# Bias rows in 24 spaced copies, one-hot rows cast by GpSimd, wider convolution ends, an earlier weight load

## The chip, the core and the metric

The kernel runs on one core of a Trainium2 chip. The core has TensorE (PE in the profile, with PEld for its weight loads), VectorE (DVE), ScalarE (ACT), GpSimd (POOL) and a sync engine (SP) that issues most of the transfers between device memory and the on-chip memory; 16 DMA engines carry them out. Each engine runs its own list of instructions in order, and waits on semaphores for the others. The metric is the time of one execution in microseconds of the device, a median of runs; lower is better.

## What is computed

One decoder block on a sequence of 1024 tokens of width 1024, in float32. Two mixers run side by side on the normalised input: dilated sliding-window attention in three groups of eight heads, with a bias that depends on the distance, and a convolution over 31 taps. Their results are gated, mixed, and followed by a feed-forward part. What the change touches is the bias and the convolution:

```python
bias = bias_tab[rel_bucket(offset * dilation)].astype(jnp.float32).transpose(2, 0, 1)
s = jnp.einsum('brnqhd,brnkhd->brnhqk', qb, kb).astype(jnp.float32) * (Dh ** -0.5) + bias
...
u, gate = jnp.split(h, 2, axis=-1)
u = u * jax.nn.sigmoid(gate)
u = lax.conv_general_dilated(u, w_dw, ..., feature_group_count=CONV_CHANNELS) + b_dw
u = jax.nn.silu(layer_norm(u, g_ln, b_ln))
return u @ w_conv_out + b_conv_out
```

## The kernel before

Every matrix product is made of two-part numbers: a float32 block is split into a high part, which ScalarE casts, and a low part, the difference, which VectorE or GpSimd computes, and three matmuls of 128x512 take the place of one (L336 to L338, L352 to L354). Most products are further done in the seven-product scheme for 2x2 blocks (`winograd`, `pair`), which needs sums of weight quarters (`quarters`, L214 to L256). So a weight block is loaded by SP (`load_ahead`, L183), split or summed by ScalarE, VectorE and GpSimd, and only then used by TensorE.

The program's order is written out by hand. TensorE's matmuls are emitted in the order of the stages, and after each group of three `tick` is called. At a tick, steps that were put off (`later`) are emitted, and each background generator goes on to its next `yield`; `yield n` lets n ticks pass and goes on at the one after. What a tick emits stands on the queue of its engine in that order, and an engine that waits holds up all that stands behind it. On SP, too, a transfer that waits holds up the transfers behind it.

The stages around the change, in order of time:

- Start, and two gated units on unsplit products; then the normalised input is prepared (`renorm`, `block_sums`) beside one early gate unit and five first halves of gated pairs (`head`, L400). The weight blocks of this stretch are split by `part` (L196 on ScalarE, L197 on VectorE); the first pair's sums are made by L236 and L237 and split by L214 and L215.
- Six gated pairs, whose results `d_u` go to memory (L887); seven pairs of gates; twelve pairs of queries and keys (`qk_pair`, L986 to L1013). Beside them `conv` computes the convolution, one block of 128 channels after the other: 46 products with accumulation (L848 to L853) in three banks, with gaps given by `CONV`; then ScalarE copies a bank (L858, L859), VectorE makes three sums (L861 to L863), the block is stored (L865), and GpSimd later adds it to a running sum (L875). L376, L904 to L917 and L1001 to L1013 empty TensorE's banks on ScalarE and VectorE and stand between these.
- The value projections (L1113, L1114), beside them the layer norm of the convolution (`conv_norm`: L1463 forms the mean from the running sum, L1472 to L1479 subtract, square and add, L469 reduces) and the attention. At its end one gate unit (`plain_gate`) and the convolution's output product with eight weight blocks `w_co`.

`bias_lines`, a background generator of the second stage, makes the bias rows: a one-hot matrix of 33x384 times the bias table gives 8 rows of 384 values per group, a `line`. The line is stored (L536) and expanded by one transfer from memory to memory, which repeats each of its 8 rows 128 times (L539, `rep`, 1.5 MB). The attention loads slanted windows of `rep` from 579 us on (L549).

Of the kernel before, what the change touches and what calls it, by code (L numbers as in the profile page):

```python
# [10 lines left out]
F32R = mybir.dt.float32r  # L11
# [53 lines left out]
class Build:  # L65
# [440 lines left out]
    def bias_lines(self):  # L506

        nc = self.nc
        self.rep = []

        def load(g):
            oh = self.slot(F32R)
            nc.gpsimd.dma_start(oh[0:33, :384], self.p_onehot[g].bitcast(F32R))
            return oh

        nxt = load(0)
        tab = self.half()
        nc.gpsimd.memset(tab[32:33, :24], 1.0)
        nc.gpsimd.dma_start(tab[0:32, :24], self.p_tab)
        yield 8  # L520
        parts = self.half(F32R)
        hi, lo = parts[0:33, :24], parts[0:33, 24:48]
        nc.scalar.copy(hi, tab[0:33, :24])
        nc.vector.tensor_tensor(lo, tab[0:33, :24], f(hi), op=OP.subtract)
        yield 8
        for g in range(3):
            oh, nxt = nxt, load(g + 1) if g < 2 else None
            ps = self.bank()
            for e, part in enumerate((hi, lo)):
                nc.tensor.matmul(ps[0:8, :384], part[:, g * 8:(g + 1) * 8], oh[0:33, :384],  # L530
                                 start=e == 0, stop=e == 1)
            oh = None
            yield 1
            nc.scalar.copy(tab[64:72, :384], ps[0:8, :384])
            line = self.dram.tile([8, 384], F32, name=f"line{g}")
            nc.sync.dma_start(line, tab[64:72, :384])  # L536
            rep = self.dram.tile([8, 128, 384], F32, name=f"rep{g}")
            yield 10
            nc.sync.dma_start(rep, bass.AP(tensor=line.tensor, offset=line.offset,  # L539
                                           ap=[[384, 8], [0, 128], [1, 384]]))  # L540
            self.rep.append(rep)
            yield 14
# [263 lines left out]
    def conv(self):  # L806
# [3 lines left out]
        nc = self.nc  # L810
# [14 lines left out]
        nxt, src = fetch(0), None  # L825
        yield 0

        for b in range(8):
# [27 lines left out]
            src = ahead  # L856
            o = self.slot()
            nc.scalar.copy(s, A[0])  # L858
            nc.scalar.copy(o[:, 0:1], A[0][:, 0:1])  # L859
            yield 1  # L860
            nc.vector.tensor_tensor(o[:, 1:H], s[:, 1:], A[1][:, :H - 1], op=OP.add)  # L861
            nc.vector.tensor_tensor(s, s, A[1], op=OP.add)
            nc.vector.tensor_tensor(o[:, H:], A[2], s, op=OP.subtract)  # L863
# [19 lines left out]
    cg, CONV = 0, (0, 1, 0, 0, 0, 1)  # L883
# [799 lines left out]
def build(ctx, tc, aps):  # L1683
    B = Build(ctx, tc, aps)
    nc = B.nc
# [73 lines left out]
    def plain_gate(n, job, early):  # L1759
        if early:  # L1760
            B.queue_split(job)
            B.flush(job)
            w = B.hl.pop(job)
        else:
            w = B.timed([job], co[:1], 3, 9)[0]
        for hf in range(2):
# [591 lines left out]
```

## Time and profile before

| what | value |
|---|---|
| median of three runs | 1688.18 us (1686.38 to 1690.43) |
| profiled execution | 1687.09 us, span 1685.3 us |
| granted TensorE clock in it | 0.999 |

The span goes from the first to the last instruction of the profiled execution. A row of the timeline gives start and length in us, engine, line, operation and tiles, how many instructions it stands for, and in brackets the idle time ahead of it with what ended it. A row of a window gives the busy time of TensorE, its weight loads, VectorE, ScalarE and GpSimd, then the clock, the share of the DMA engines and GB/s. TensorE's busy time is modelled from its instructions, so its gaps are read from the idle times.

### The profile page before, as it was taken

The numbers are of one execution on the slowest core, as the hardware profiler recorded it, in microseconds if no ns is written. First come the engines' busy times: TensorE is split into PE (matmuls) and PEld (weight loads), VectorE is DVE, ScalarE is ACT, GpSimd is POOL, SyncE is SP. The second block draws the span as 40 slices with busy tenths as digits, with TensorE's granted clock in tenths as the row PEclk, the third lists the DMA queues.
The fourth block names the chain that finished last, engine by engine and source line by source line (L and its number), as shares of the span: only waits on it lengthen the run. The fifth ranks groups of instructions, "written<-read, shape, count | busy, mean of one in ns | idle before, by whom it ended". The sixth has DMA issues, their size and how long they took to land.

```text
span 1685.3 us, 23529 instructions
## 1 busy us (share of the span) xinstructions
PE 1668.1 (99%) x8119; PEld 1393.9 (83%) x8119; DVE 1277.7 (76%) x2268; ACT 827.6 (49%) x1646; POOL 522.2 (31%) x408
## 2 busy tenths in 40 slices
PE   9999999999999999999999999999999999999998
PEld 7778888888878889999888888888888888888886
DVE  6899988888988767778885846877655566676686
ACT  7354334343444588888822447643333333354453
POOL 0028777888777165665300300000000000000000
PEclk9999999999999999999999999999999999999999
DMA  4443343355656888779998624234133222494334
GB/s 182 164 165 138 110 140 119 138 186 174 197 166 171 269 269 236 225 233 256 308 274 316 198 88 153 74 131 150 69 107 118 94 94 106 170 374 126 111 121 156
DMA packets 164641, 289.66 MB, mean 172 GB/s; under 512 B 47534, under 2 KB 79273, under 8 KB 164521
## 3 DMA queue, kind: packets, MB, share of 16 engines
q1 hardware_dynamic: 163832, 287.56, 52.6%
q8 instruction: 64, 1.05, 0.3%
q0 software_dynamic: 544, 0.34, 0.1%
q14 instruction: 57, 0.46, 0.1%
q10 hardware_dynamic: 144, 0.26, 0.0%
HBM read 197.39 MB, written 95.42 MB: 174 GB/s over the span
## 4 chain that ended last, share of the span: by engine, by line
PE 67%; DMA 3%; DVE 1%; ACT 1%; issue 0%; SPq 0%; DVEq 0%; POOL 0%; POOLq 0%; ACTq 0%
PE p L2242 12%; PE p L353 10%; PE p L354 10%; PE p L352 10%; PE p L1986 5%; PE p L1113 5%; PE p L1114 3%; PE p L336 2%; PE p L338 2%; PE p L337 2%; PE p L1229 2%; PE p L1300 2%; PE p L1267 1%; DMA b<-dk 1%; DMA b<-dq 1%; DMA b<-dv 0%
## 5 line engine op out<-in xcount | busy, mean ns | idle before, releaser
L352 PE MATMUL p<-b,b 128*128 128x512 f32 x1316 | 513.6, 390 | 3.5 <-ACT b L214 1.7
L354 PE MATMUL p<-b,b 128*128 128x512 f32 x1316 | 512.8, 390 | 0.9 <-DVE b L215 0.5
L353 PE MATMUL p<-b,b 128*128 128x512 f32 x1316 | 512.2, 389 | 0.1
L352 PEld LDWEIGHTS p<-b,b 128*128 128x128 f32 x1316 | 247.0, 188 | 58.6 <-ACT b L214 2.1
L354 PEld LDWEIGHTS p<-b,b 128*128 128x128 f32 x1316 | 247.0, 188 | 54.4 <-DVE b L197 1.5
L353 PEld LDWEIGHTS p<-b,b 128*128 128x128 f32 x1316 | 247.1, 188 | 51.4 <-DVE b L1437 0.5
L2242 PE MATMUL p<-b,b 128*128 128x512 f32 x924 | 209.6, 389 | 0.0
L2242 PEld LDWEIGHTS p<-b,b 128*128 128x128 f32 x924 | 173.5, 188 | 36.0
L853 DVE SCALAR_TENSOR_TENSOR p<-b,par,p 128x511 f32<-128x511 f32 (+14 forms) x232 | 163.2, 738 | 0.0
L1113 PE MATMUL p<-b,b 128*128 128x512 f32 x384 | 144.1, 407 | 0.0
L214 ACT CAST b<-d 128x1024 fp32r<-128x1024 f32 x82 | 86.2, 1051 | 97.3 <-POOL d L237 54.5
L215 POOL TENSOR_TENSOR b<-d,b 128x1024 fp32r<-128x1024 f32 x43 | 104.6, 2433 | 50.7 <-ACT b L214 38.9
L1437 DVE TENSOR_TENSOR b<-b,b 128x512 fp32r<-128x512 f32 x141 | 98.8, 707 | 16.9 <-ACT b L1436 15.3
L215 DVE TENSOR_TENSOR b<-d,b 128x1024 fp32r<-128x1024 f32 x39 | 47.6, 1220 | 79.3 <-ACT b L214 79.3
L1114 PE MATMUL p<-b,b 128*128 128x256 f32 x384 | 107.7, 280 | 0.0
L1436 ACT CAST b<-b 128x512 fp32r<-128x512 f32 x141 | 86.4, 619 | 39.7 <-PE p L2242 18.1
L336 PE MATMUL p<-b,b 128*128 128x512 f32 x240 | 96.1, 401 | 0.0
L338 PE MATMUL p<-b,b 128*128 128x512 f32 x240 | 93.6, 390 | 0.0
L337 PE MATMUL p<-b,b 128*128 128x512 f32 x240 | 93.6, 390 | 0.0
L214 ACT CAST b<-b 128x1024 fp32r<-128x1024 f32 x51 | 53.6, 1052 | 80.4 <-POOL b L246 36.5
L1242 ACT ACTIVATE c<-c,stat 128x128 f32<-128x128 f32 (+1 forms) x192 | 85.2, 448 | 14.6 <-DVE stat L1232 13.3
L1986 PE MATMUL p<-b,b 128*128 128x512 f32 x384 | 90.0, 392 | 0.0
(245 smaller groups left out, 2879.1 us busy)
## 6 DMA issues: line engine op xcount, KB each, us to landing
b<-w_in SPq DMA_DIRECT2D x33, 512.0 KB, 5.0
b<-w_fi SPq DMA_DIRECT2D x29, 512.0 KB, 5.0
d<-w_in SPq DMA_DIRECT2D x25, 512.0 KB, 4.4
dk<-c SPq DMA_DIRECT2D x48, 256.0 KB, 4.1
dq<-c SPq DMA_DIRECT2D x48, 256.0 KB, 3.8
b<-dq SPq DMA_DIRECT2D x48, 256.0 KB, 5.6
b<-dk SPq DMA_DIRECT2D x48, 256.0 KB, 7.3
d<-w_fi SPq DMA_DIRECT2D x22, 512.0 KB, 4.1
```

What stands on the lines that cost most here:

```text
L214: self.nc.scalar.copy(hi, x)
L215: self.wsplit.tensor_tensor(lo, x, f(hi), op=OP.subtract)
L336: nc.tensor.matmul(ps, hi[:, s], a, start=kt == 0, stop=False)
L337: nc.tensor.matmul(ps, hi[:, s], b, start=False, stop=False)
L352: nc.tensor.matmul(ps, hi[:, s], a, start=first and kt == 0, stop=False, skip_group_check=True)
L353: nc.tensor.matmul(ps, hi[:, s], b, start=False, stop=False, skip_group_check=True)
L354: nc.tensor.matmul(ps, lo[:, s], a, start=False, stop=kt == 3, skip_group_check=True)
L853: nc.vector.scalar_tensor_tensor(A[i][:, j:], src[i][:, :H - j], w[i], A[i][:, j:], op0=OP.mult, op1=OP.add)
L1113: nc.tensor.matmul(ps, a, w, start=kt == 0, stop=kt == KT - 1, skip_group_check=True)
L1114: nc.tensor.matmul(ps[:, 256:], b, w[:, :256], start=False, stop=kt == KT - 1, skip_group_check=True)
L1986: nc.tensor.matmul(banks[tt][nh], st, wt[:, nh * H:(nh + 1) * H], start=bool(kt == 0 and a), stop=bool(kt == KT - 1 and b))
L2242: nc.tensor.matmul(acc[t], x, y, start=first and e == 0, stop=last and e == 2, skip_group_check=True)
```

## The change

Four edits. `bias_lines` loads its one-hot rows by SP as float32 into smaller tiles, and GpSimd casts them to the type that TensorE takes, where before GpSimd's own queue loaded them straight into tiles of that type. It stores the three lines early, frees its tiles, lets 60 ticks pass, and then expands each line in eight transfers of one row each, four ticks apart. `conv` lets three ticks pass ahead of the copies of a finished bank, three ahead of the sums, and puts the sums on ticks of their own; the gaps between its products are shorter on average at first (`CONV` as set in the class; the list set for the query and key pairs stays). In `plain_gate` the load of the second `w_co` block is set to 14 ticks after the start of the late gate unit.

```diff
-        def load(g):
-            oh = self.slot(F32R)
-            nc.gpsimd.dma_start(oh[0:33, :384], self.p_onehot[g].bitcast(F32R))
-            return oh
-
-        nxt = load(0)
+        oh = []
+
+        def load(g):
+            x = self.half()
+            nc.sync.dma_start(x[0:33, :384], self.p_onehot[g])
+            oh.append(x)
+
+        load(0)
         tab = self.half()
         nc.gpsimd.memset(tab[32:33, :24], 1.0)
         nc.gpsimd.dma_start(tab[0:32, :24], self.p_tab)
-        yield 8
+        yield 6
...
-        yield 8
+        load(1)
+        lines = []
         for g in range(3):
-            oh, nxt = nxt, load(g + 1) if g < 2 else None
+            x, y = oh.pop(0), self.half(F32R)
+            nc.gpsimd.tensor_copy(y[0:33, :384], x[0:33, :384])
+            x = None
+            if g == 0:
+                load(2)
+            yield 5
             ps = self.bank()
             for e, part in enumerate((hi, lo)):
-                nc.tensor.matmul(ps[0:8, :384], part[:, g * 8:(g + 1) * 8], oh[0:33, :384],
+                nc.tensor.matmul(ps[0:8, :384], part[:, g * 8:(g + 1) * 8], y[0:33, :384],
                                  start=e == 0, stop=e == 1)
-            oh = None
-            yield 1
+            y = None
+            yield 2
             nc.scalar.copy(tab[64:72, :384], ps[0:8, :384])
+            ps = None
             line = self.dram.tile([8, 384], F32, name=f"line{g}")
             nc.sync.dma_start(line, tab[64:72, :384])
+            lines.append(line)
+        tab = parts = hi = lo = line = part = None
+        yield 60
+        for g, line in enumerate(lines):
             rep = self.dram.tile([8, 128, 384], F32, name=f"rep{g}")
-            yield 10
-            nc.sync.dma_start(rep, bass.AP(tensor=line.tensor, offset=line.offset,
-                                           ap=[[384, 8], [0, 128], [1, 384]]))
+            for h in range(8):
+                nc.sync.dma_start(rep[h], bass.AP(tensor=line.tensor, offset=line.offset + h * 384,
+                                                  ap=[[0, 128], [1, 384]]))
+                yield 3
             self.rep.append(rep)
-            yield 14
...
             src = ahead
+            yield 2
             o = self.slot()
             nc.scalar.copy(s, A[0])
             nc.scalar.copy(o[:, 0:1], A[0][:, 0:1])
-            yield 1
+            yield 2
             nc.vector.tensor_tensor(o[:, 1:H], s[:, 1:], A[1][:, :H - 1], op=OP.add)
+            yield 0
             nc.vector.tensor_tensor(s, s, A[1], op=OP.add)
+            yield 0
             nc.vector.tensor_tensor(o[:, H:], A[2], s, op=OP.subtract)
...
-    cg, CONV = 0, (0, 1, 0, 0, 0, 1)
+    cg, CONV = 0, (0,0,0,1)
...
             w = B.timed([job], co[:1], 3, 9)[0]
+            B.later(14, lambda: B.load_ahead(co[1]))
```

The edits add lines, so the change's line numbers are higher: L515 and L531 load and cast the one-hot rows, L545 stores a line and L552 expands it, L829 is the old L816 and L903 the old L887; L866 is a tap, L875, L877 and L879 are the three sums, L881 the block's store, and the old L986 to L1013 are 16 higher.

SP's queue in the stretch of the five first halves, before: `line`, then weight blocks, and the expansion of group 0 between them.

```order
L1737 DMA du_90<-b_603 128x1024
L183 DMA b_727<-w_in 128x1024
L536 DMA line_748<-c_632 8x384
L887 DMA dgc_128<-c_763 128x512
L183 DMA b_774<-w_in 128x1024
L539 DMA rep_750<-line_748 1024x1x384
L887 DMA dgc_128<-c_803 128x512
L816 DMA b_806<-du_89 128x1024
L183 DMA b_823<-w_in 128x1024
L183 DMA b_878<-w_in 128x1024
L183 DMA d_900<-w_in 128x1024
```

The same place now:

```order
L1753 DMA du_90<-b_603 128x1024
L545 DMA line_734<-c_632 8x384
L183 DMA b_741<-w_in 128x1024
L903 DMA dgc_128<-c_771 128x512
L183 DMA b_782<-w_in 128x1024
L545 DMA line_786<-c_632 8x384
L903 DMA dgc_128<-c_818 128x512
L829 DMA b_821<-du_89 128x1024
L183 DMA b_838<-w_in 128x1024
L545 DMA line_845<-c_632 8x384
L183 DMA b_896<-w_in 128x1024
L183 DMA d_918<-w_in 128x1024
```

The expansion has gone from here, and all three lines are stored here. The first of the new transfers stand behind the store of `d_u` block 2, among the weight blocks of the gated pairs:

```order
L903 DMA du_91<-c_1190 128x512
L552 DMA rep_1223<-line_734 128x384 x3
L183 DMA d_1280<-w_in 128x1024
L183 DMA b_1282<-w_in 128x1024
L552 DMA rep_1223<-line_734 128x384 x2
L903 DMA du_92<-c_1194 128x512
L903 DMA du_92<-c_1316 128x512
L552 DMA rep_1223<-line_734 128x384 x2
L829 DMA b_1378<-du_90 128x1024
```

From here on they go on in this way, one to four together, to the last gated pair.

VectorE's queue at the end of a convolution block among the query and key pairs (in the trace at 407 to 414 us), before:

```order
L987 TENSOR_TENSOR c_3602<-c_3602,c_3625 128x512
L861 TENSOR_TENSOR b_3620<-c_3039,p_3127 128x511
L862 TENSOR_TENSOR c_3039<-c_3039,p_3127 128x512
L863 TENSOR_TENSOR b_3620<-p_3128,c_3039 128x512
L850 TENSOR_SCALAR p_3643<-b_3371,par 128x512
L848 TENSOR_SCALAR p_3644<-b_3371,par 128x512
L850 TENSOR_SCALAR p_3645<-c_3572,pairs,bias_551 128x512
L1007 TENSOR_TENSOR c_3671<-p_3548,c_3552 128x128x4
```

And the end of the same block now:

```order
L1003 TENSOR_TENSOR c_3702<-c_3702,c_3721 128x512
L1029 SCALAR_TENSOR_TENSOR c_3725<-p_3567,c_3724 128x128x4
L875 TENSOR_TENSOR b_3748<-c_3126,p_3228 128x511
L877 TENSOR_TENSOR c_3126<-c_3126,p_3228 128x512
L879 TENSOR_TENSOR b_3748<-p_3229,c_3126 128x512
L1017 TENSOR_TENSOR c_3781<-p_3729,c_3730 128x128x4
L863 TENSOR_SCALAR p_3786<-b_3486,par 128x512
L861 TENSOR_SCALAR p_3787<-b_3486,par 128x512
L1003 TENSOR_TENSOR c_3781<-c_3781,c_3805 128x512
L863 TENSOR_SCALAR p_3788<-c_3670,pairs,bias_551 128x512
```

The block ends later against the pairs, and instructions that empty TensorE's banks (L1017) stand between the sums and the first products of the next block. At another block the order is again sums, one product, then L1023, the old L1007.

VectorE's queue at the end of the last block, before; behind it come a pair without taps and then the value projections:

```order
L853 SCALAR_TENSOR_TENSOR p_4164<-c_4086,par,p_4164 128x497
L1007 TENSOR_TENSOR c_4649<-p_4535,c_4539 128x64x8
L861 TENSOR_TENSOR b_4654<-c_4086,p_4163 128x511
L862 TENSOR_TENSOR c_4086<-c_4086,p_4163 128x512
L863 TENSOR_TENSOR b_4654<-p_4164,c_4086 128x512
L990 SCALAR_TENSOR_TENSOR c_4649<-c_4649,c_4669 128x512
L1001 TENSOR_TENSOR c_4672<-p_4607,c_4538 128x64x8
L987 TENSOR_TENSOR c_4672<-c_4672,c_4690 128x512
L1013 SCALAR_TENSOR_TENSOR c_4694<-p_4535,c_4693 128x64x8
```

And now, up to the last L1029 (the old L1013) ahead of the value projections:

```order
L866 SCALAR_TENSOR_TENSOR p_4336<-c_4231,par,p_4336 128x497
L208 TENSOR_TENSOR b_4817<-b_4728,b_4817 128x2x256
L1023 TENSOR_TENSOR c_4820<-p_4707,c_4711 128x64x8
L208 TENSOR_TENSOR b_4837<-b_4730,b_4837 128x2x256
L1006 SCALAR_TENSOR_TENSOR c_4820<-c_4820,c_4840 128x512
L1017 TENSOR_TENSOR c_4843<-p_4779,c_4710 128x64x8
L875 TENSOR_TENSOR b_4831<-c_4231,p_4335 128x511
L877 TENSOR_TENSOR c_4231<-c_4231,p_4335 128x512
L208 TENSOR_TENSOR b_4859<-b_4730,b_4859 128x2x256
L879 TENSOR_TENSOR b_4831<-p_4336,c_4231 128x512
L1003 TENSOR_TENSOR c_4843<-c_4843,c_4863 128x512
L1029 SCALAR_TENSOR_TENSOR c_4867<-p_4707,c_4866 128x64x8
```

The last block now ends in the last pair instead of the one before it: 15 taps that stood ahead of the old end of the block, and the three sums, stand between the last L1007 of the pair before and the last L1013. GpSimd's addition of the block, L875 before, stands behind them. On SP, the store of block 7 stood well ahead of the loads for the layer norm and now stands behind the first of them; and the second `w_co` block, which stood behind two `dq` loads, a store and two `dact` loads, now stands ahead of them.

## The prediction

> **What bounds the kernel now.** I read the page's head and the busy time by window first, then TensorE's own timeline for every gap, and from each gap back to what released it.
>
> ```profile
> span 1685.3 us, 23529 instructions
> PE 1668.1 (99%) x8119; PEld 1393.9 (83%) x8119; DVE 1277.7 (76%) x2268; ACT 827.6 (49%) x1646; POOL 522.2 (31%) x408
> ...
> 50.00:100.00 50.00, 47.41 (x201) 35.88 (x199) 44.81 (x73) 22.46 (x40) 1.04 (x2) 1.00 0.51 181
> 400.00:500.00 100.00, 98.51 (x430) 80.09 (x429) 91.29 (x118) 41.18 (x60) 79.85 (x46) 1.00 0.59 180
> 800.00:900.00 100.00, 97.57 (x526) 81.72 (x525) 82.62 (x177) 46.59 (x132) 17.83 (x23) 1.00 1.00 290
> ```
>
> TensorE is the bound: it is busy for 1668.1 of 1685.3 us and the change keeps every large matmul. So only its 17.2 us of gaps can be won. Three windows hold most of what lies inside the program: 2.59, 1.49 and 2.43 us (window minus the PE column). These are the gaps themselves; the bracket gives the idle time and its releaser:
>
> ```profile
> 89.39 0.50 PE L354 MATMUL p<-b,b 128*128 128x512 f32 x1 [0.28 <-DVE b L197]
> 96.67 0.50 PE L352 MATMUL p<-b,b 128*128 128x512 f32 x1 [1.67 <-ACT b L214]
> 97.92 0.50 PE L354 MATMUL p<-b,b 128*128 128x512 f32 x1 [0.53 <-DVE b L215]
> ...
> 413.37 0.50 PE L352 MATMUL p<-b,b 128*128 128x512 f32 x1 [0.59 <-DVE c L1007]
> 468.63 0.50 PE L352 MATMUL p<-b,b 128*128 128x512 f32 x1 [0.56 <-ACT c L376]
> 472.00 0.50 PE L352 MATMUL p<-b,b 128*128 128x512 f32 x1 [0.35 <-DVE c L1007]
> ...
> 809.99 0.39 PE L1300 MATMUL p<-c,b 128*128 128x256 f32 x1 [1.02 <-ACT c L1274]
> ```
>
> **Part A, the bias rows: 2.5 us won.** The first three gaps have one cause, a late weight block.
>
> ```profile
> 66.05 0.77 SPq L539 DMA_DIRECT2D rep<-line  x1
> 71.77 0.89 SPq L183 DMA_DIRECT2D b<-w_in  x2
> 81.98 0.62 ACT L196 CAST b<-b 128x512 fp32r<-128x512 f32 x1 [5.17 <-DMA b<-w_in]
> 82.63 0.69 DVE L197 TENSOR_TENSOR b<-b,b 128x512 fp32r<-128x512 f32 x1 [4.23 <-ACT b L196]
> 94.07 0.69 DVE L236 TENSOR_TENSOR d<-b 128x512 f32<-128x512 f32 x1
> 95.57 1.04 ACT L214 CAST b<-d 128x1024 fp32r<-128x1024 f32 x1 [3.10 <-DVE d L237]
> b<-w_in SPq DMA_DIRECT2D x33, 512.0 KB, 5.0
> ```
>
> The load issued at 71.77 lands at 81.98, 10.2 us later, where such loads take 5.0 in the median. ACT waits 5.17 us for it, VectorE 4.23 behind ACT. VectorE's queue is then full; L236 runs late, L214 and L215 behind it, and TensorE stands 0.28 + 1.67 + 0.53 = 2.48 us. What the load met is the 1.5 MB expansion issued at 66.05. The change takes all three expansions out of this stretch. The load then lands near 76.8, when ACT had finished its earlier work (81.98 - 5.17). I take 2.5; the ends are 0 (something else holds the load) and the window's 2.59.
>
> What it adds there: three 49.5 KB loads behind the first store of `du`, on a queue that then waits for VectorE anyway; three line stores, each a queue entry ahead of a weight load; and three GpSimd casts, on an engine that was busy 1.04 us in the whole window. A 64-row cast of 512 columns gives an upper price:
>
> ```profile
> 805.70 0.60 POOL L1053 CAST b<-b 64x512 fp32r<-64x512 f32 x1
> ```
>
> By the code's gaps a one-hot load stands seven ticks ahead of its cast and the cast six ticks ahead of its matmul. A tick is three matmuls, 0.69 us by the second window (3 x 98.51 / 430), so load and cast have 8.9 us together; a 512 KB load lands in 5.0 and the cast takes 0.6 at most. Nothing is charged; if the cover went, a late cast would cost TensorE up to its 0.6 us.
>
> The 24 pieces now run from about 113 us on, 3 to 8 per pair of weight blocks, each one queue entry of 196 KB. While an old expansion ran, the DMA engines looked like this (85 to 100 us, forty slices):
>
> ```profile
> DMA  1000000555559955589999995555545455410000
> ```
>
> Half of the engines are busy for some 29 slices of 0.375 us, 10.9 us, where nothing is added. A piece is an eighth of that work: 1.4 us at this rate. By the code a weight block is loaded there 15 ticks, 10 us, ahead of its first cast and lands in 5.0, so three pieces in front are absorbed: 0 charged. Nothing waits for the pieces themselves before the attention, some 400 us on. The upper end is that the stall of A returns once, 2.5. The Trainium skill, page "DMA: Bandwidth & Descriptors", section "Why a DMA increments its semaphore by 16 and not by 1", says a copy runs on as many engines, up to 16, as divide the slowest dimension of both sides: 8 for the old form, 16 for a piece. The half-busy row agrees; by the rule a piece takes 0.7 us instead of 1.4, which leaves the sum alone and lowers the chance of the second rival below.
>
> **Part B, the convolution's ends: 1.1 us won.** At a block's end ACT copies a finished bank (L858) and VectorE adds three times without a pause.
>
> ```profile
> 412.28 1.04 DVE L1007 TENSOR_TENSOR c<-p,c 128x512 f32<-128x512 f32 x1
> 467.44 0.59 ACT L858 COPY c<-p 128x512 f32<-128x512 f32 x1 [2.24 <-DVE p L853]
> 467.98 0.60 ACT L376 COPY c<-p 128x512 f32<-128x512 f32 x1
> 470.88 1.06 DVE L1007 TENSOR_TENSOR c<-p,c 128x512 f32<-128x512 f32 x1
> ```
>
> At 467 the copy had been queued before its last tap was done; L376, which frees TensorE's bank, stood 2.24 us behind it: 0.56 us of TensorE. At 412 and 471 L1007 stood behind the three sums and the next block's first products: 0.59 and 0.35. The three extra ticks ahead of the copy remove the first kind; spacing the sums lets L1007 in between, though the change's order still has one block where L1007 follows the sums directly. Of 1.50 I take 1.1; ends 0 and 1.5.
>
> **Part C, the second w_co load: 1.0 us won.**
>
> ```profile
> 792.16 0.54 SPq L1038 DMA_DIRECT2D b<-dq  x1
> 798.75 1.40 SPq L183 DMA_DIRECT2D b<-w_co  x2
> 806.90 0.62 ACT L196 CAST b<-b 128x512 fp32r<-128x512 f32 x1 [1.30 <-DMA b<-w_co]
> 809.46 0.48 ACT L1274 CAST c<-p 128x384 fp32r<-128x384 f32 x1
> DMA to landing us min/median/max: 5.8/8.5/11.2
> ```
>
> ACT waits 1.30 us for this block, so L1274 is 1.30 late and TensorE stands 1.02. The load moves to just behind the row at 792.16, 6 us earlier; even with the slowest landing of the eight, 11.2 us, it is there by 804, before ACT asks at 805.6. It passes two `dq` loads and two `dact` loads, which come about 1.8 us later (512 KB at the window's 290 GB/s); the `dq` blocks are used by GpSimd's copies, which run at 805.70 in the row above, 10 us after. I take 1.0; ends 0 and 1.02.
>
> **Part D, the convolution's last block: 1.0 us lost.** The wider ends cost more ticks than the quicker taps save, so block 7 ends a third of a pair from the attention projections instead of a pair. Between L1007 at 527 and the last L1013, 15 taps are new on VectorE.
>
> ```profile
> L853 DVE SCALAR_TENSOR_TENSOR p<-b,par,p 128x511 f32<-128x511 f32 (+14 forms) x232 | 163.2, 738 | 0.0
> 533.26 1.87 DVE L987 TENSOR_TENSOR c<-c,c 128x512 fp32r<-128x512 f32 x1 [0.69 <-ACT c L986]
> 537.93 1.11 DVE L1001 TENSOR_TENSOR c<-p,c 128x512 f32<-128x512 f32 x1 [1.79 <-issue]
> 541.73 1.32 DVE L987 TENSOR_TENSOR c<-c,c 128x512 fp32r<-128x512 f32 x1 [2.69 <-ACT c L986]
> 542.97 3.49 DVE L208 TENSOR_TENSOR b<-b,b 128x512 fp32r<-128x512 f32 x2
> 552.60 1.08 DVE L1013 SCALAR_TENSOR_TENSOR c<-p,c 128x512 fp32r<-128x512 f32 x1 [1.36 <-ACT c L1012]
> 542.45 2.86 POOL L875 TENSOR_TENSOR b<-b,b 128x1024 f32<-128x1024 f32 x1
> 554.79 1.88 PE L1463 MATMUL p<-b,mean_col 128*128 128x512 f32 x4
> 578.63 5.91 DVE L1478 TENSOR_TENSOR b<-b,b 128x1024 f32<-128x1024 f32 x3
> 585.48 1.84 PE L469 MATMUL p<-mean_col,b 128*128 128x1 f32 x16
> ```
>
> A tap starts about 0.65 us after the one before (738 ns overlap a little): 9.8 us. The idle time there is 0.69 + 1.79 + 2.69 + 1.36 = 6.5, so 3.3 us are over. The two L208 of 3.49 us ran beside GpSimd's L875; that sum now comes later, and at the 0.6 from start to start that such a split takes alone (L197's row is one) they give back 2.3. VectorE is then 1.0 us late at L1013. L1013 ended at 553.68 and the matmul that waits for it stands shortly ahead of L1463 at 554.79, so I count half of that distance as slack: 0.5 us of stall. L875 starts only behind the last sum, which stands two rows ahead of L1013, so L1463 is late by about as much and not in addition. The store of block 7 now stands among the normalisation's loads on SP and waits for that sum; I estimate that it holds three of them for 2 us. The chain that ends at 584.54 (L1478) has 0.9 us before L469 needs it: 1.1 late, of which the first stall hides half: 0.5. Together 1.0; the ends are 0 and 3.3 + 0.9 = 4.2.
>
> The Trainium skill, page "SBUF — State Buffer", section "Who interferes with whom", says that a VectorE instruction with two SBUF inputs and a GpSimd instruction that reads SBUF shut each other out for a whole instruction. The 3.49 us of the two L208 agree; if their length were their own and nothing came back, D would be 3.3 and the sum 1.3 less, 1686.9.
>
> **Sum.** 2.5 + 1.1 + 1.0 - 1.0 = 3.6 us less. The profiled execution took 1687.09, so it gives 1683.5; the median of the runs, 1688.18, lies 1.09 above, so 1684.6.
>
> **Rivals.**
> - B fails: the 24 new order changes (copies, sums and evacuations fall in other places in all eight blocks) make as many gaps as they remove. VectorE at 91.29 of 100 us speaks for it; the wait of 2.24 us, which the ticks plainly cure, against. 2.5 + 1.0 - 1.0 = 2.5 less: 1685.7.
> - The transfers aren't hidden: the pieces meet weight loads of the paired stretch and one stall like A's returns, so the expansion only moves its price. For: VectorE has no slack there. Against: the loads are issued long before their use. 3.6 - 2.5 = 1.1 less: 1687.1.
> - Slower: the last block. The 6.5 us of idle time are waits for ACT's L986 and L1012; if taps put into them only push these chains, VectorE is 9.8 us late at L1013 and TensorE, with the 0.5 of slack, waits 9.3. 9.3 - 4.6 = 4.7 more: 1692.9. It decides from 4.6 us of lateness at 554 on. Against: most of the idle time is VectorE waiting, which a tap can fill.
>
> **Chances.** Forecast 0.55, B fails 0.22, transfers 0.11, last block 0.12. A measurement of this kernel can tell about 0.2%, 3.4 us, so faster means under 1684.8; my own number lies just under it. Of the forecast's 0.55 I give 0.44 to faster, and 0.06 from the second case, whose better half crosses: 0.50. Slower is the last case, 0.12; the rest, 0.38, is the same. The range goes from 1681.8 (all of A, B and C, 5.1, no loss, and 1.3 for the scatter of the runs) to 1688.9 (the transfers' case and 1.8 of scatter); the last block's case lies outside.
>
> **What would show it.** A: no wait of ACT for `w_in` between 60 and 90, no TensorE gap from 85 to 100. B: no gap of TensorE on L376 or L1007 after a copy or the sums. C: ACT's wait for `w_co` and the gap of 1.02 gone. D: a new gap ahead of L1463 near 550 and one at L469, each under 1 us. I am wrong if new gaps appear between 113 and 190 where the pieces run, or if TensorE stands more than 2 us at the change of stage near 550.

## The result, and the profile after

| | before | after |
|---|---|---|
| median | 1688.18 us (1686.15 to 1692.77, 17 runs) | 1684.17 us (1681.35 to 1686.92, 17 runs) |
| ratio after / before | | 0.9973, 95% interval 0.9964 to 0.9981 |
| profiled execution | 1687.09 us, span 1685.3 | 1683.92 us, span 1682.1 |

By the ratio the change makes the kernel 4.6 us faster (interval 3.2 to 6.1), where 3.6 was forecast; the two medians differ by 4.0. The head of the page, and then three windows of the changed kernel that answer to those shown of before (time, then the busy time of TensorE, weight loads, VectorE, ScalarE and GpSimd, clock, DMA share, GB/s):

```profile
span 1682.1 us, 23547 instructions
PE 1666.9 (99%) x8119; PEld 1394.4 (83%) x8119; DVE 1272.9 (76%) x2268; ACT 828.1 (49%) x1646; POOL 525.8 (31%) x408
...
50.00:100.00 50.00, 49.80 (x218) 39.63 (x217) 49.04 (x79) 24.91 (x45) 1.67 (x2) 1.00 0.35 125
400.00:500.00 100.00, 99.69 (x437) 81.47 (x436) 87.25 (x114) 43.49 (x63) 80.29 (x46) 1.00 0.60 180
800.00:900.00 100.00, 97.54 (x520) 81.57 (x519) 82.55 (x170) 47.49 (x131) 16.03 (x21) 1.00 0.96 289
```

The first two windows have lost their gaps, 2.59 to 0.20 and 1.49 to 0.31 us. The third hasn't: 2.43 before, 2.46 now. TensorE's timeline, the rows with idle time behind the first 60 us:

```profile
121.03 0.50 PE L352 MATMUL p<-b,b 128*128 128x512 f32 x1 [0.88 <-DVE c L925]
158.09 0.50 PE L354 MATMUL p<-b,b 128*128 128x512 f32 x1 [0.70 <-POOL b L215]
425.19 0.50 PE L352 MATMUL p<-b,b 128*128 128x512 f32 x1 [0.30 <-ACT c L371]
551.30 0.51 PE L1129 MATMUL p<-b,b 128*128 128x512 f32 x1 [0.25 <-DVE c L1029]
552.56 1.98 PE L1479 MATMUL p<-b,mean_col 128*128 128x512 f32 x4 [0.29 <-POOL b L891]
...
809.36 0.28 PE L1316 MATMUL p<-c,b 128*66 128x128 f32 x1 [0.53 <-DVE c L1291]
815.72 0.42 PE L1245 MATMUL p<-b,b 128*128 128x128 f32 x2 [0.97 <-DMA b<-dk]
```

Five of these are new or larger: 121 (0.26 before), 158, the two near 552, and a wait for a `dk` block at 816 where the wait behind the `w_co` block (1.02) had been.

**A stall costs more than its idle time.** By the heads of the two pages TensorE's idle time (the span without its busy time) went from 17.2 to 15.2 us, yet the span is 3.2 shorter. Before, near 97 us:

```profile
94.60 0.40 PE L354 MATMUL p<-b,b 128*128 128x512 f32 x1
96.67 0.50 PE L352 MATMUL p<-b,b 128*128 128x512 f32 x1 [1.67 <-ACT b L214]
97.01 0.39 PE L353 MATMUL p<-b,b 128*128 128x512 f32 x1
97.92 0.50 PE L354 MATMUL p<-b,b 128*128 128x512 f32 x1 [0.53 <-DVE b L215]
98.27 0.40 PE L352 MATMUL p<-b,b 128*128 128x512 f32 x1
```

Undisturbed, these matmuls start every 0.226 us (443 in 100 us). From 94.60 to 96.67 are 2.07 us, 1.84 too many, where 1.67 is printed; and the next start comes 0.34 later instead of 0.23. Waits too short to be printed add to it. So what a stretch cost is read from when a fixed instruction starts. I use four marks, all rows of TensorE's timeline: the first L336 (42.97 us before, 43.91 after), the first value projection (551.27, 548.08), the first product of the attention's weights with the values (621.35, 618.69) and the last one beside the gate unit (845.24, 842.44). The table gives how much longer (+) or shorter each kernel of this study took between marks than the kernel before did, in its one profiled execution; the median and the ratio to before come from all its runs.

| kernel | to 43 | 43 to 551 | 551 to 621 | 621 to 845 | median us (runs) | ratio, 95% interval |
|---|---|---|---|---|---|---|
| the change | +0.94 | -4.13 | +0.53 | -0.14 | 1684.17 (17) | 0.9973 (0.9964 to 0.9981) |
| after_again | -1.02 | -4.20 | +1.06 | +0.32 | 1684.76 (12) | 0.9977 (0.9967 to 0.9988) |
| only_bias | -1.25 | -3.76 | 0.00 | +1.41 | 1682.06 (5) | 0.9963 (0.9951 to 0.9975) |
| only_bias_2 | -0.39 | -3.73 | -0.01 | -0.31 | 1682.32 (5) | 0.9962 (0.9949 to 0.9976) |
| only_conv | -0.22 | +2.03 | +3.20 | +0.02 | 1691.91 (11) | 1.0024 (1.0016 to 1.0033) |
| only_wco | -0.69 | -0.48 | +0.01 | +0.53 | 1687.01 (11) | 0.9995 (0.9985 to 1.0005) |
| bias_wco | -0.76 | -3.80 | +0.01 | +0.58 | 1683.09 (12) | 0.9976 (0.9967 to 0.9986) |
| conv_bank_t | +0.04 | +2.28 | +0.55 | +0.09 | 1687.79 (10) | 1.0003 (0.9994 to 1.0012) |
| after_bank_t | -0.51 | -0.98 | +2.24 | +0.68 | 1687.75 (10) | 0.9999 (0.9988 to 1.0009) |
| rep_whole_late | -0.18 | -4.10 | +0.57 | +4.65 | 1684.57 (10) | 0.9976 (0.9966 to 0.9986) |
| rep_split_early | +0.73 | -4.08 | +0.52 | -1.18 | 1683.97 (8) | 0.9975 (0.9965 to 0.9985) |
| bias_wco_dgc | +0.57 | -3.75 | 0.00 | -0.32 | 1683.05 (6) | 0.9969 (0.9957 to 0.9981) |
| after_dgc | +0.68 | -4.15 | +0.54 | +0.37 | 1684.12 (6) | 0.9971 (0.9960 to 0.9983) |

One execution of `only_wco`, 2792 us at a mean clock of 0.556, is left out of its row.

In `only_conv` and `after_bank_t` the mark at 551 stands behind a gap of 3 us, which so falls into the second column. Apart from that, the second and third column repeat within 0.12 us among the kernels with the bias edit and the same convolution, with one exception (1.06); without the bias edit the second scatters. The first scatters by 2 us whatever the kernel: the matmuls there are the same in all, and TensorE waits for the splits of its first weight blocks by amounts that change from one execution to the next. Behind the last mark the ten profiles with the bias edit take 839.5 to 839.7 us to the end of the span, and the four without it 840.0 to 840.1. So the edit saves another 0.4 us, all of it behind VectorE's last instruction; what saves it is not shown.

### The profile page after: what moved, and what is told of

The parts are those of the page before. It is cut to its first block, busy times and chain, and to the rows that moved or that the text cites. A ratio compares the mean times of both kernels' runs of the same rounds, so it can differ in the third digit from the quotient of the medians.

```text
span 1682.1 us, 23547 instructions
## 1 busy us (share of the span) xinstructions
PE 1666.9 (99%) x8119; PEld 1394.4 (83%) x8119; DVE 1272.9 (76%) x2268; ACT 828.1 (49%) x1646; POOL 525.8 (31%) x408
## 4 chain that ended last, share of the span: by engine, by line
PE 86%; issue 5%; POOL 3%; DMA 3%; DVE 2%; ACT 1%; SPq 0%; DVEq 0%; POOLq 0%; ACTq 0%
PE p L353 15%; PE p L352 15%; PE p L354 15%; PE p L2259 12%; PE p L2003 5%; PE p L1129 5%; PE p L1130 3%; PE p L336 2%; PE p L338 2%; PE p L337 2%; PE p L1245 2%; PE p L1316 2%; PE p L1283 2%; PE p L653 1%; POOL b L215 1%
## 5 line engine op out<-in xcount | busy, mean ns | idle before, releaser
L866 DVE SCALAR_TENSOR_TENSOR p<-b,par,p 128x511 f32<-128x511 f32 (+14 forms) x232 | 163.7, 737 | 0.0
L214 ACT CAST b<-d 128x1024 fp32r<-128x1024 f32 x82 | 86.2, 1051 | 102.4 <-POOL d L237 58.1
L215 POOL TENSOR_TENSOR b<-d,b 128x1024 fp32r<-128x1024 f32 x43 | 104.4, 2428 | 45.7 <-ACT b L214 38.4
L1453 DVE TENSOR_TENSOR b<-b,b 128x512 fp32r<-128x512 f32 x141 | 98.6, 705 | 16.9 <-ACT b L1452 15.3
L215 DVE TENSOR_TENSOR b<-d,b 128x1024 fp32r<-128x1024 f32 x39 | 47.6, 1221 | 79.3 <-ACT b L214 79.3
L336 PE MATMUL p<-b,b 128*128 128x512 f32 x240 | 96.3, 401 | 0.0
L214 ACT CAST b<-b 128x1024 fp32r<-128x1024 f32 x51 | 53.6, 1052 | 82.8 <-POOL b L246 41.1
```

What stands on the lines that cost most here:

```text
L214: self.nc.scalar.copy(hi, x)
L215: self.wsplit.tensor_tensor(lo, x, f(hi), op=OP.subtract)
L336: nc.tensor.matmul(ps, hi[:, s], a, start=kt == 0, stop=False)
L866: nc.vector.scalar_tensor_tensor(A[i][:, j:], src[i][:, :H - j], w[i], A[i][:, j:], op0=OP.mult, op1=OP.add)
```

## The experiments

### Each part alone, and the change once more

To the kernel before, `only_bias` adds the new `bias_lines`, as in the change's diff. `only_conv` has the new waits in `conv` and the new `CONV`, of which the first and the last lines are

```diff
+            yield 2
             o = self.slot()
             nc.scalar.copy(s, A[0])
...
-    cg, CONV = 0, (0, 1, 0, 0, 0, 1)
+    cg, CONV = 0, (0,0,0,1)
```

and `only_wco` one line in `plain_gate`:

```diff
             w = B.timed([job], co[:1], 3, 9)[0]
+            B.later(14, lambda: B.load_ahead(co[1]))
```

`after_again` is the changed kernel.

> The kernel before with the edit of the bias rows alone. Theory: the three printed gaps between 89 and 98 us (2.48 us of idle time) cost more than their idle time, since TensorE also starts 0.1 us later than its 0.23 us beat for some matmuls behind each; measured from start to start the stretch 70 to 105 us lost 4.2 us more before than with the change, so this edit alone gives 3.5 to 4.2 us, ratio near 0.9977, and no new gap at 121 or 158 us. Rival 1 (the prediction's term): 2.5 us, ratio 0.9985. Rival 2 (the pieces make the new gaps that the changed kernel has at 121 us, 0.88, and 158 us, 0.70): both stand in this profile too, and the gain is 1.4 us less, some 2.5.

Measured: -3.76 between the marks at 43 and 551, so the theory holds there and the prediction's 2.5 was too small. The gaps at 121 and 158 us are 0.21 and none, so the pieces don't make them. The share of the theory that names the whole time falls: the median is 6.0 us lower, not 4.

> The bias edit alone once more, to see whether its 1682.06 (5 runs) stands. Theory: the rest of the change is worth nothing within 1 us (block ends +1.7, new gaps -1.4, last block -0.5, w_co 0), so the median lies at 1683 to 1684.5 like those of bias_wco and of the change, ratio 0.9972. Rival: the convolution's edit costs 2 us beside it, and the median stays near 1682, ratio 0.9964. The profile has the gap for L1287 behind the w_co block again, between 1 and 2.7 us, and no dk gap.

Measured: 1682.32, the rival's number. The bias edit alone is at least as fast as the whole change: its ten runs, 1681.7 to 1684.2, have a median of 1682.3, where the change has 1684.5 in 29. That speaks for 2 us that the rest of the change costs; but the two intervals of the ratio overlap, and most of the 2 us goes with the clock of the runs (below). The expected gap for L1287 came with 0.72 us, under the forecast's 1.

> The kernel before with the convolution's edit alone (waits around a block's end, and the denser list of gaps). Theory: the gaps at 121 and 158 us and the two near 551 us come from this edit, since a denser convolution puts products on VectorE and a block's first addition on GpSimd ahead of what TensorE waits for; they cost 1.4 and 0.5 us, the gaps at 413, 469 and 472 us go and give 1.7, so the edit is worth 0 within 0.5 us, ratio 1.000. Rival: the gaps near 121 and 158 us aren't there, and the edit wins 0.6 to 1.5 us, ratio 0.9993.

Measured: both failed. The edit alone makes the kernel 4.1 us slower by the ratio. The new gaps at 121 and 158 us are there (0.92 and 0.70), as the theory had it, but what it expected near 551 us was far too little. The profile shows where, with TensorE's row and windows from 548 us on:

```profile
553.08 0.79 PE L1116 MATMUL p<-b,b 128*128 128x512 f32 x1 [3.03 <-DVE c L1016]
```

```profile
548.00:552.00 4.00, 2.05 (x10) 1.36 (x8) 3.97 (x8) 1.68 (x2) 0.37 (x1) 1.00 0.80 205
552.00:556.00 4.00, 2.92 (x9) 2.53 (x10) 1.02 (x2) 0.00 (x0) 2.31 (x1) 0.52 1.02 391
556.00:560.00 4.00, 4.00 (x15) 3.19 (x14) 0.00 (x0) 0.59 (x1) 0.00 (x0) 0.63 0.98 342
```

TensorE waited 3.03 us for the last L1016 (L1013 before, L1029 in the change), and then ran at half its clock: the column behind the engines is 0.52 and 0.63. In the table the two columns together are +5.23. The same late instruction costs the changed kernel a gap of 0.25. The difference is a bank. In `only_conv` the first value projection is given the bank which that L1016 empties; in the change and in the kernel before, the first one gets a bank that TensorE's own earlier products left free, and the second one, whose first product comes 2.8 us later (eight pairs of products, 0.35 us each), gets the late one. Up to there the two programs differ in nothing but `bias_lines`, which takes three banks and gives them back at other times.

> The kernel before with the second w_co load moved alone. Theory: the DMA engines are busy for the whole stretch from 786 to 822 us, so an earlier block makes later ones late: the gap of 1.02 us for L1274 goes and one of about 1 us for a dk block near 815 us comes; nothing is won, ratio 1.000 within 0.0003. Rival (the prediction's term): the gap goes and none comes, 1.0 us won, ratio 0.9994, to be read from the gaps of the profile between 800 and 845 us.

Measured: the theory. The gap for L1274 is gone, and another has come:

```profile
811.00 0.27 PE L1300 MATMUL p<-c,b 128*66 128x128 f32 x1 [0.53 <-DVE c L1275]
817.86 0.42 PE L1229 MATMUL p<-b,b 128*128 128x128 f32 x2 [1.47 <-DMA b<-dk]
```

The time is the same within its interval.

> The changed kernel once more, to see how far its gaps repeat. Theory: the gaps at 121, 158, 425, 551, 816 us repeat within 0.2 us; the first stage, which began 0.95 us later than in the profile of before (gaps of 0.51, 0.59 and 0.31 for weight splits), varies between executions. Rival: the late first stage belongs to the changed kernel and comes again with the same 0.9 us. Time 1684.2 within 1.5, ratio 0.9973.

Measured: the gaps came again as 0.87, 0.70, 0.25, 0.24 with 0.29, and 1.15 us at 816. The late start did not: -1.02 where the first profile had +0.94. It is scatter.

### The bank

The edit is one line, to each of two kernels. A pool gives its tags their banks in the order in which they are first asked for.

```diff
     B.bank("s")
+    B.bank("t")
```

> The convolution's edit alone, as in only_conv, with one line more: a bank of tag t is allocated behind the one of tag s, so that the first value projection takes a bank that an earlier pair left, and the second one the bank that the last L1016 empties. Theory: the loss of only_conv lies in the bank order. There TensorE waited 3.03 us for that L1016 at the first value projection, and the granted clock then was 0.50 from 553 to 559 us, which cost 2.8 more; here the second projection asks some 2.8 us later, the gap is under 0.5 us, the clock stays at 1.00, and the time is 5.8 us below only_conv's 1691.9: 1686.1, ratio 0.9988. Rival: the loss lies in VectorE's work and not in the bank; the gap moves to another matmul and the time stays within 2 us of 1691.9, ratio 1.002.

> The changed kernel with the same line, which here does the opposite: the first value projection takes the bank that the last L1029 empties. Theory: TensorE waits about 3.2 us there (in the changed kernel the first value projection began at 548.1 and L1029 ended at 551.25), the granted clock halves for about 6 us, and the time rises by 5.5 us to 1689.8, ratio 1.0010. Rival 1: the wait comes without the lower clock, +2.9 us, 1687.2, ratio 0.9994. Rival 2: the bank doesn't matter, 1684.3, ratio 0.9976.

First `conv_bank_t`, then `after_bank_t`, the row with the gap and two windows each:

```profile
556.82 0.50 PE L1116 MATMUL p<-b,b 128*128 128x512 f32 x1 [0.25 <-DVE c L1016]
```

```profile
552.00:556.00 4.00, 4.00 (x22) 3.40 (x21) 3.97 (x7) 1.74 (x2) 0.68 (x1) 1.00 0.88 238
556.00:560.00 4.00, 3.45 (x13) 1.81 (x12) 0.76 (x1) 1.17 (x2) 2.02 (x1) 1.00 0.98 348
```

```profile
549.78 0.80 PE L1129 MATMUL p<-b,b 128*128 128x512 f32 x1 [3.02 <-DVE c L1029]
```

```profile
548.00:552.00 4.00, 2.22 (x7) 1.94 (x8) 1.72 (x3) 0.00 (x0) 2.68 (x1) 0.64 1.00 366
552.00:556.00 4.00, 4.00 (x14) 3.42 (x13) 0.00 (x0) 0.59 (x1) 0.00 (x0) 0.51 0.99 374
```

The line takes the wait out of the one kernel and puts it into the other, with the clock. The bank decides. By the medians it is worth 4.1 us to `only_conv` (5.8 expected) and costs the change 3.0 to 3.6 (5.5 expected). In the profile of `after_bank_t` the stages around it lose 4.9 against the change (-0.98 + 2.24 against -4.13 + 0.53).

By its runs `conv_bank_t` is as fast as the kernel before (1.0003), and 1.7 us slower than expected. Its profiled execution took longer, 1690.09 us, and met a worse form of the old stall: a gap of 1.31 more at 84 us, then 0.28, 1.71 and 0.53, and behind them a clock of 0.57:

```profile
96.00:100.00 4.00, 1.76 (x7) 1.00 (x7) 3.97 (x6) 2.33 (x4) 0.00 (x0) 1.00 0.42 164
100.00:104.00 4.00, 4.00 (x12) 2.25 (x11) 4.00 (x7) 2.59 (x5) 0.00 (x0) 0.57 0.00 0
```

In windows of a tenth of a microsecond the clock is 0.50 from 100.2 to 103.5 us. The kernel before has gaps of 1.67 and 0.53 in the same places, and keeps 1.00 behind them (`only_conv` and `only_wco`, 1.70 and 0.53, too):

```profile
100.00:104.00 4.00, 4.00 (x19) 3.14 (x18) 4.00 (x7) 3.35 (x6) 0.00 (x0) 1.00 0.00 0
```

How often this happens can be read from the mean clock that the record has for every run. The nine profiles in which the clock falls only behind TensorE's last products have a mean of 0.999. The two with 3.4 us more at half clock (`conv_bank_t`, and `rep_split_early` from 7.3 to 10.8 us) have 0.998, and the three with 6.8 us more 0.997. Of the 88 runs of the kernel before that were taken beside the experiments, only 29 have 0.999 (median 1686.4); 44 have 0.998 (1688.2) and 15 less. Of the change's 29 runs 18 have 0.999 (1683.5), of `only_bias`'s ten runs all (1682.3). So at the same mean clock the bias edit is worth 4.1 us, as in its profiles (3.75 and the 0.4 behind the last mark), and the rest of its 6 us goes with the lower clock, which none of its runs met. Which stall lowers it in the runs of the kernel before is not shown, since a mean does not say where.

Four of the ten runs of `after_bank_t` have 0.999 or 0.998, the other six 0.997 or 0.996, so its clock did not fall in all of them as in the profile; in `only_conv` all eleven have 0.997 or 0.996. That fits its median, 1687.75, which is nearer to rival 1's 1687.2 than to the theory's 1689.8, though the profile shows the theory's mechanism.

### Moving, or spacing, the expansions

`rep_whole_late` puts one transfer for each group back in place of the eight, late. `rep_split_early` keeps the 24 pieces and takes the delay away.

```diff
-            for h in range(8):
-                nc.sync.dma_start(rep[h], bass.AP(tensor=line.tensor, offset=line.offset + h * 384,
-                                                  ap=[[0, 128], [1, 384]]))
-                yield 3
+            nc.sync.dma_start(rep, bass.AP(tensor=line.tensor, offset=line.offset,
+                                           ap=[[384, 8], [0, 128], [1, 384]]))
+            yield 31
```

```diff
-        yield 60
+        yield 1
```

> The changed kernel with each group's expansion as one transfer again, as in before, but still late: one every 32 ticks from where the pieces begin. Theory: what helped is that the expansions left the stretch before 100 us, where each weight block is loaded shortly ahead of its use; in the pairs' stretch the loads stand 10 us ahead, so the whole form does no harm: no wait of ACT or GpSimd for a w_in block between 110 and 190 us, no new gap, 1684.5, ratio 0.9976. Rival: the split matters; a whole expansion that runs for 10.9 us on half of the engines holds a weight block up by some 5 us there as well, and a gap of 1 to 2.5 us comes back once or more: 1686 to 1688, ratio 0.9985 to 1.000.

> The changed kernel without the 60 ticks of delay ahead of the expansions: the 24 pieces, four ticks apart, run from about 70 us to 140 us, through the stretch that the change had emptied. Theory: a weight block waits for what stands ahead of it in the transfers; a piece is an eighth of the old one, so no load is held for more than 1.5 us, and the stretch from 70 to 105 us loses under 1 us against the changed kernel: 1684.5 to 1685.3, ratio 0.9980. Then the spacing alone would have done it. Rival: the place decides; the loads there have no slack, three or more gaps come back, 2.5 to 4 us: 1687 to 1688.5, ratio 0.9995.

Either suffices. The stretch from 65 to 105 us, in the kernel before, in the change and in `rep_split_early`:

```profile
65.00:105.00 40.00, 37.41 (x157) 27.98 (x156) 35.74 (x59) 22.04 (x40) 0.52 (x1) 1.00 0.56 199
```

```profile
65.00:105.00 40.00, 39.97 (x175) 32.23 (x174) 39.93 (x65) 24.02 (x42) 0.00 (x0) 1.00 0.41 148
```

```profile
65.00:105.00 40.00, 39.98 (x175) 32.22 (x174) 39.93 (x65) 24.20 (x42) 0.00 (x0) 1.00 0.61 214
```

TensorE starts 175 matmuls there instead of 157; 18 times 0.226 are 4.1 us. With the pieces in this very stretch it carries more bytes than before (214 against 199 GB/s) and no gap returns: it was not the bytes in this place that hurt, but the whole expansion ahead of the loads. And as one transfer but late, ahead of loads that have 10 us to spare, it does no harm either: -4.10 and the change's own gaps, no more. Both runs keep the rest of the bias edit (the one-hot loads by SP, the early stores of the lines), and none tried the eight pieces together in the old place. So whether the size of the old transfer, its half of the engines or its place in the queue delayed the load is not shown. In the profile of `rep_whole_late` the last column is +4.65, from a wait for a `dk` block of another size:

```profile
817.26 0.66 PE L1244 MATMUL p<-b,b 128*128 128x128 f32 x2 [3.65 <-DMA b<-dk]
```

```profile
816.00:820.00 4.00, 2.73 (x11) 2.37 (x11) 3.38 (x14) 1.83 (x7) 0.00 (x0) 0.50 1.06 379
```

Again a gap over 3 us, and again half the clock. The edit touches nothing near it, and the median of its ten runs is the change's.

### The stretch where the transfers are the limit

`bias_wco` leaves the convolution as it was. The other two also set the load of the second `dgc` block later, which is issued at 799 us and first used at 824:

```diff
-            nxt = gate_load(B.d_gc[n + 1]) if n < 7 else (gate_load(B.d_ga[0]), gate_load(B.d_gc[0]))
+            nxt = gate_load(B.d_gc[n + 1], 0 if n else 4) if n < 7 else (gate_load(B.d_ga[0]), gate_load(B.d_gc[0]))
```

In the changed kernel, on SP's timeline, that load stands ahead of the `dk` blocks:

```profile
798.25 0.33 SPq L183 DMA_DIRECT2D b<-w_co  x1
799.32 0.32 SPq L1908 DMA_DIRECT2D b<-dgc  x1
801.41 1.09 SPq L1060 DMA_DIRECT2D b<-dk  x2
803.03 0.33 SPq L1906 DMA_DIRECT2D b<-dgc  x1
804.37 1.09 SPq L1060 DMA_DIRECT2D b<-dk  x2
```

> The kernel before with the bias rows and the second w_co load edited, the convolution untouched. Theory: the convolution's edit is worth nothing beside the bias edit (it wins 1.7 us at block ends, loses 1.4 at 121 and 158 us and 0.5 near 551), and the low median of only_bias is scatter of its five runs: 1683.5 to 1684.5, ratio 0.9975. Rival: the convolution's edit costs some 2 us beside the bias edit too: 1682, ratio 0.9964. In the profile the wait for the w_co block, 2.68 us in only_bias, is gone and one for a dk block of 1.0 to 1.5 us is there, so from 778 to 845 us it loses 0.5 us against before, where only_bias lost 1.65.

> The changed kernel with the load of the second dgc block, 512 KB that VectorE uses only near 824 us, set four ticks later, so that it stands behind four dk loads and a rep window instead of ahead of them. Theory: between 786 and 822 us the transfers are the limit (DMA engines busy throughout, all profiles with the moved w_co load show TensorE waiting for a dk block near 816 us, 0.97, 1.15, 1.47, 1.52, 1.81 and once 3.65 us); half a megabyte less ahead of the dk blocks, 1.7 us at the window's 296 GB/s, removes that gap or cuts it to under 0.3, and the time falls by 1 us or a little more: 1683, ratio 0.9968. Rival: the dk block is late for another reason (its slot, or its place on the queue) and the gap of about 1 us stays: 1684.3, ratio 0.9976.

> The bias edit, the moved w_co load and the later dgc load, with the convolution of before. Theory: no gap for w_co, dk or L1274 over 0.5 us between 800 and 830 us, the gaps at 413, 469 and 472 us as before, none at 158 or 551; 1 us below bias_wco's 1683.1: 1682, ratio 0.9967, the fastest of all. Rival: the transfers' limit only moves on, to a dact, dv or datt block, and the time is bias_wco's: 1683, ratio 0.9975.

Measured: `bias_wco` has the `w_co` wait replaced by one of 1.52 for `dk`; its median lies between the two forecasts. In `after_dgc` the `dk` gap is gone, and one of 1.43 for L1291 stands at 823.73 us instead. There VectorE's L1453, ahead of L1291, took 1.76 us where another one takes 0.68, beside GpSimd's L1101; GpSimd had waited for a `dv` block until 820.51 us (819.97 in the change, where no L1453 ran beside L1101):

```profile
817.60 0.68 DVE L1453 TENSOR_TENSOR b<-b,b 128x512 fp32r<-128x512 f32 x1
821.59 1.76 DVE L1453 TENSOR_TENSOR b<-b,b 128x512 fp32r<-128x512 f32 x1
821.20 1.59 POOL L1101 TENSOR_TENSOR b<-b,b 128x512 fp32r<-128x512 f32 x1
```

In `bias_wco_dgc` 0.72 of the `dk` gap is left. The medians, 1684.12 and 1683.05, are those without the edit, as the rival has it. That the `dk` gap is gone in `after_dgc` can't be put down to the edit either: `rep_split_early`, with the moved `w_co` load and without this edit, has no gap for `w_co` or `dk`, and none near 824 us, in its profile. What this stretch costs differs between executions more than between kernels. `only_bias` has no edit there, and lost 1.41 us in one profile, with a gap of 2.68 behind the `w_co` block, and gained 0.31 in the other, with 0.72.

`only_bias` and the two kernels with `bias_wco` in their names lie 1 to 2 us below the change; at a mean clock of 0.999 alone (1682.3 for `only_bias`, 1683.5 for the change) the difference of 1.2 us is within the scatter of the runs.

## Why the prediction was right

The total was right, 3.6 us forecast and 4.6 (3.2 to 6.1) measured. But none of its four terms had its forecast size, and their errors cancelled: A's gain was too small, B's and C's too large, D's loss too large. The clock, for which the prediction has no term, adds to the measured gain: at a mean clock of 0.999 the change and the kernel before are 2.8 us apart (1683.5 and 1686.4), and 18 of the change's 29 runs keep this clock where 29 of 88 of before did. So the cause of A was foreseen, and that the total agrees is in part luck.

- **A, 2.5 us: right cause, size too small.** ACT's waits for `w_in` from 60 to 90 us fell from 10.6 to 1.1 us, where the prediction's last part asked for none, and the three gaps are gone, as it asked. The term was sized by printed idle time; from mark to mark it is 3.75, and another 0.4 behind the last mark. That nothing would be charged for the pieces held: `only_bias` has no new gap between 105 and 190 us, and ahead of the first one-hot matmul stands a gap of 0.20. New gaps between 113 and 190 us, which the prediction named as a sign of being wrong, did come in the change (0.88 at 121, 0.70 at 158), but not from the pieces: `only_bias` has the pieces and not these gaps, `only_conv` the gaps and not the pieces. What I hadn't counted, ACT's two waits for the line stores (7.9 us), cost TensorE nothing. That no gap returned when the pieces ran early also says that the rival "transfers not hidden" was far off.
- **B, 1.1 us: the gaps went, and new ones took most of it back.** 0.59, 0.56 and 0.35 became one of 0.30. But the denser list of gaps also moves the convolution against the pairs, and here the rival that has B fail, with as many new gaps as old, was mostly right. At 121 us one tap more stands ahead of L925 than stood ahead of the old L909. At 158, GpSimd's first addition of a block has moved ahead of two weight sums. First before, then after:

```profile
152.63 1.30 POOL L245 TENSOR_TENSOR b<-d,b 128x512 f32<-128x512 f32 x1
153.88 1.75 POOL L246 TENSOR_TENSOR b<-d,d 128x512 f32<-128x512 f32 x1
155.59 1.48 POOL L822 TENSOR_TENSOR c<-b 128x512 f32<-128x512 f32 x1
```

```profile
149.92 1.05 POOL L835 TENSOR_TENSOR c<-b 128x512 f32<-128x512 f32 x1
150.92 1.87 POOL L245 TENSOR_TENSOR b<-d,b 128x512 f32<-128x512 f32 x1
152.75 1.74 POOL L246 TENSOR_TENSOR b<-d,d 128x512 f32<-128x512 f32 x1
```

  The split behind them, L214 and L215, is late by that, and TensorE waits 0.70. Between 43 and 551 us the convolution's edit is left with some 0.35 (-4.08 to -4.20 with it, -3.73 to -3.80 without). I had looked for what the pauses cure and had priced the new order at the block ends only. Whether the pauses or the new `CONV` makes these two gaps wasn't tried apart.
- **C, 1.0 us: wrong.** The block was early enough and its gap went, but I had let the `dq` and `dact` loads behind it be 1.8 us later at no cost and not looked at `dk`. The step that failed took the landing times of the old order, 5.8 to 11.2 us, as given and let an earlier issue cost the others nothing. With the DMA share at 1.00 the wait moved to a `dk` block in six of the seven profiles that have the moved load without the later `dgc` (0.97 to 1.81 us, once 3.65); in the seventh, `rep_split_early`, TensorE waited for neither block. `only_wco`, the run of this edit alone, is the same in time.
- **D, 1.0 us lost: half of it, 0.53.** The gap for the last sum came as forecast (0.25), and L1479 waits behind GpSimd's L891 (0.29), which I had counted as no addition. The one at L469 never came. The two L208 of 3.49 us did fall back when GpSimd's sum moved away from them:

```profile
541.26 0.68 DVE L208 TENSOR_TENSOR b<-b,b 128x512 fp32r<-128x512 f32 x1
543.15 0.68 DVE L208 TENSOR_TENSOR b<-b,b 128x512 fp32r<-128x512 f32 x1
```

  By the Trainium skill, page "SBUF — State Buffer", section "Who interferes with whom", the two engines shut each other out there; the trace agrees, and the case in which nothing came back falls.
- **The slower rival** had the place right and the mechanism in part: L1013 late at the change of stage. I had it decided by how late VectorE is, from 4.6 us on. The runs show that 3.0 us of TensorE's idle time there cost about 5, that in the change too L1029 ended 3.2 us (551.25 against 548.08) behind the first value projection's start, and that the bank given to the first value projection decides. The change escaped it by the side effect of another of its edits, which nothing in the prediction had looked for.

Sum of the terms as measured between the marks: 3.75 + 0.35 + 0 - 0.53 = 3.6, and with the 0.4 behind the last mark, which no term had, 4.0.

## What to carry to other kernels

Count what a stall cost from one fixed instruction to the next, with undisturbed spacing beside it, and not from the printed idle time; read the mean clock of every run beside its time; and test the parts of a change alone, since a right total here held a term half as large again, one of nothing and one that came out at a third. Where TensorE goes from one stage into the next, look at which bank the first products are given and who empties it last: one line that changes the order of the banks moved the time by 3 to 4 us, up in one kernel and down in the other. Where the DMA engines are busy throughout, look at what a load passes before moving it ahead: here the wait moved to another load in six profiles of seven.

## What the hardware showed that I had not expected

Gaps of 3.03, 3.02 and 3.65 us each ended with TensorE at half its granted clock. In windows of a tenth of a microsecond the clock went to 0.50 some 2.1 to 2.3 us into the gap in all three and stayed there for 6.8 us, 5.5 to 6.1 of them with TensorE busy again. A single gap of 2.68 did not do it. Behind gaps of 1.71 and 0.53 us within three the clock fell once, for 3.4 us, half as long; behind the same two gaps it stayed at 1.00 in three other profiles, so their length alone does not decide. The Trainium skill, page "TensorE: Matmul & The Clock Gate", section "Why this matters for your kernels", warns of idle gaps of more than about 3 us, because one idle window returns the array to half rate. The three rows over 3 us agree. Falls behind shorter gaps, as in `conv_bank_t`, and in `rep_split_early` at 7.3 us behind gaps of 0.41 and 0.90, are not in that rule. A gap just over 3 us cost about 5 here.
